# A decoder layer on one core: the last three value blocks worked quarter by quarter with a pre-summed second tile, gathered rows that end earlier, and four PSUM rooms for the queries

## The chip, the cores and the metric

The kernel runs on one core of a Trainium2 chip. The metric is device time in microseconds of one execution. The core has five engines with queues of their own: TensorE (PE, with its weight loads shown as PEld), VectorE (DVE), ScalarE (ACT), GpSimd (POOL) and SyncE (SP). DMA transfers are issued from the queues of SP and POOL here, and 16 DMA engines carry them.

## The reference, cut to what matters

One layer over 256 tokens of width 2048, in float32. An attention and retention part comes first (the first 575 us here, untouched by the change). Then a PEER block: product-key retrieval picks 16 of 16384 single-neuron experts for each of 8 heads of a token, so 128 experts a token.

```python
q = (hf @ w_q).reshape(T, PEER_HEADS, 2, PEER_QUERY_DIM // 2)
s_half = jnp.einsum('thpd,hpkd->thpk', q, sub_keys).astype(F32)
v_half, i_half = lax.top_k(s_half, K)
cand_s = (v_half[:, :, 0, :, None] + v_half[:, :, 1, None, :]).reshape(T, PEER_HEADS, K * K)
cand_i = (i_half[:, :, 0, :, None] * PEER_N_KEYS + i_half[:, :, 1, None, :]).reshape(T, PEER_HEADS, K * K)
top_s, pick = lax.top_k(cand_s, K)
experts = jnp.take_along_axis(cand_i, pick, axis=-1)
gates = jax.nn.softmax(top_s, axis=-1)
...
    a = jnp.einsum('cd,ced->ce', hc, w_u[ec]).astype(F32)
    coef = (gc * jax.nn.gelu(a)).astype(dt)
    return jnp.einsum('ce,ced->cd', coef, w_v[ec])
...
    x = x + gate2 * peer_ffn(h2, peer_w_q[l], peer_sub_keys[l], peer_u[l], peer_v[l])
return rmsnorm(x, g_norm_final)
```

## The kernel before

**Two ways to the experts.** Tokens 0 to 191 (TD = 192) go the dense way: all 16384 experts are computed on PE, and a matrix X holds gate times activation, which is zero for experts that a token didn't pick. The last 64 tokens (NS) go the sparse way: their 128 chosen rows are gathered from HBM by indirect DMAs on POOL, one 128x2048 tile a step, and DVE multiplies. Tokens 160 to 191 take their activations by gathering too (NM = 32). In all there are 160 steps: 32 "m", 64 "u" and 64 "v". They run beside the dense work, and `sparse(n)` says how many are due at a block; `STEPS` lists the blocks for three of the four dense stages. `most` is how many gathers may be in flight, `spare` and `other` are the rooms that they land in.

**Stages.** The expert matrices go in two halves of 64 blocks of 128 experts: first activation stage (`u_half`, hf = 0), first value stage (`v_group`, hf = 0), second activation stage, second value stage. Before them lies the query stage: 16 blocks of the query projection (`t_block`), each into a PSUM bank named by `bank("A")`, which goes round banks 6 and 7; then scores and top-16 on DVE.

**A value block (j).** SP loads 1 MB into one of five `raw` tiles (L148). ACT copies it, rounded, into `hi` (L946), DVE writes the rest, `lo = raw - hi` (L947). The block's slice of X is split likewise into `cc`: `ch` (L941), `cl` (L942) and a second copy of a part of `cl` (L948); `cc` has three buffers. PE then does 20 matmuls of 512 columns (L964) into eight accumulators, `acc[(t, q)]`, for token tile t and column quarter q, one PSUM bank each: three for a quarter of the first tile (hi by hi, hi by cl, lo by hi), two for a quarter of the second, whose rows 0 to 63 and 64 to 127 are two parts of the same 64 tokens and have to be added to each other at the end ("folded"). The first half's result waits in SBUF as `s2`.

**The end.** The last NL = 3 blocks are written by quarter: all of the nine (or six) matmuls of a quarter, then that quarter's finish. Blocks 62 and 63 have `hi` and `lo` in tiles of their own (`pair`). For the second tile the finish is `te = acc + s2` on DVE (L988, one buffer), two fp32 products with a 0/1 matrix `sel`, which fold the gathered rows' sum `sp` into rows 64 to 127 (L990) and `te` into rows 0 to 63 (L991), then, for both tiles, times the gate `g2` (L992), added to x in `z` (L993), squared and summed on ACT (L995), times `gf` (L996). After the fourth quarter of a tile follow the reciprocal root (L214, L215 on DVE, L220 on POOL), the scaling by it (ACT L1002, DVE L1004) and four output transfers on SP (L1005). `z` is the tile that held the activations' input; its two halves serve as rooms for gathers in the second value stage, and x is loaded into it from DRAM late (L929, on POOL). For the first tile `s2` is multiplied by `g2` (L931) and added to `z` (L933) ahead.

**What sets the order.** Program order gives priorities, and a list scheduler with a simulated timeline fixes the order of instructions on every engine before the program runs. Instructions passed through `pin` (`inorder` is `pin` from the fourth block on) keep their written order among themselves: the loads, ACT's copies for a block, the gathers and their DVE steps. Engines then run their queues strictly in that order. A tile is written again only when its last reader is done.

Of the kernel before, what the change touches and what calls it, by code (L numbers as in the profile page):

```python
# [9 lines left out]
F32 = mybir.dt.float32  # L10
# [34 lines left out]
             u1=[j for j in range(HALF - 8) if j % 3 != 1])  # L45
# [70 lines left out]
def body(ctx, tc, a, out, dbg=None, stop=None):  # L116
# [627 lines left out]
    with ExitStack() as gctx:  # L744
# [152 lines left out]
        def v_group(hf, s2, late, fin=None):  # L897
# [3 lines left out]
            with tc.tile_pool(name=f"vsb{hf}", bufs=1) as vb:  # L901
# [5 lines left out]
                if hf:  # L907

                    sel = vb.tile([P, 3 * NS], F32, name="sel")
                    nc.vector.memset(sel, 0.0)  # L910
                    nc.vector.tensor_add(sel[:, NS:2 * NS], ident[:, 0:NS], ident[:, NS:P])
                    z = x2
                    ss = vb.tile([P, 2, 4], F32, name="ss2")

                tail = HALF - (NL if hf else 1)
                last = []
                for j in range(HALF):
                    if hf == 1:
                        if j == 44:
                            other[0], most[0] = None, 2  # L920
                        elif j == 48:
# [3 lines left out]
                        elif j == 50:  # L925
                            most[0] = 1
                        elif j in (56, 57):
                            t = j - 56
                            nc.gpsimd.dma_start(z[:, t, :], x2d[:, t, :])  # L929
                        elif j == 58:  # L930
                            nc.vector.tensor_mul(s2[:, 0, :], s2[:, 0, :], g2)  # L931
                        elif j == 60:
                            nc.vector.tensor_add(z[:, 0, :], z[:, 0, :], s2[:, 0, :])  # L933
# [3 lines left out]
                    cc = gp_.tile([P, 2 * TD + NS], F32R, name="cc", bufs=3)  # L937
                    ch, cl = cc[:, 0:TD], cc[:, TD + NS:]

                    inorder = pin if j > 2 else lambda i: i  # L940
                    inorder(nc.scalar.copy(ch, xb(j)))  # L941
                    nc.vector.tensor_sub(cl, xb(j), ch.bitcast(F32))  # L942
# [4 lines left out]
                    nc.vector.tensor_sub(lo, r, hi.bitcast(F32))  # L947
# [15 lines left out]
                    def mul(c, jj, n, x, w, m):  # L963
                        nc.tensor.matmul(acc[c][0:m], x, w[:, c[1] * 512:(c[1] + 1) * 512], start=jj == 0 and n == 0,  # L964
                                         stop=jj == HALF - 1 and n == 2 - c[0], skip_group_check=True)

                    if j < HALF - 1:
# [6 lines left out]
                        continue  # L974
# [341 lines left out]
```

## Time and profile before

| | us |
|---|---|
| median of 3 runs (range) | 1890.0 (1884.99 to 1891.03) |
| the profiled execution, own time | 1895.85 |
| its span, first to last instruction | 1894.1 |
| PE busy | 1816.1 |
| DVE busy | 1479.9 |
| ACT busy | 708.7 |
| POOL busy | 379.5 |

All times inside the execution are counted from the start of the span. 0 to 575 is the attention part, 575 to 735 the queries, then the four expert stages begin at about 735, 986, 1279 and 1571. Every matmul of the activation stages is shown as two instructions, and so is each product with `sel`: they are float32. An instruction's duration includes its fill and drain, so several that follow each other start closer together than they last.

### The profile page before, as it was taken

Reading aid. Unit: us, or ns where it says so; the run is one execution under the profiler, and the core shown is the slowest. Engines: PE = TensorE matmul, PEld = TensorE weight load, DVE = VectorE, ACT = ScalarE, POOL = GpSimd, SP = SyncE. Lnnn points to the kernel's source line nnn. Section 1 sums busy time; section 2 is a strip of 40 time slices with the busy share of each in tenths; the row PEclk is TensorE's granted clock in tenths of the full one; section 3 lists DMA queues with packets and bytes.
Section 4 is the critical chain, followed back from the end, with each engine's and each line's share of the span. In section 5 each row is a group of like instructions: output and inputs, shape, how many; then the busy total and the mean of one; then the engine's idle time right before and its main releaser. Section 6 shows DMA issues by size and latency. Waiting matters only on the chain.

```text
span 1894.1 us, 28604 instructions
## 1 busy us (share of the span) xinstructions
PE 1816.1 (96%) x11303; PEld 1589.3 (84%) x11303; DVE 1479.9 (78%) x2333; ACT 708.7 (37%) x1279; POOL 379.5 (20%) x256
## 2 busy tenths in 40 slices
PE   5899999999997999999999999999999999999995
PEld 4899878788786899999997777779999997777773
DVE  7988877879788998778388999974455559888875
ACT  3444453625434422011035545541111114555552
POOL 1000001002001002111124444421111125544210
PEclk9999899989998999999999999999999999999998
DMA  8989876879887979999889999989989979999981
GB/s 350 388 323 373 309 274 231 311 258 349 298 321 276 339 278 342 424 395 355 356 320 406 422 417 413 416 337 425 367 330 355 366 301 421 422 413 387 383 294 45
DMA packets 94473, 652.93 MB, mean 345 GB/s; under 512 B 11409, under 2 KB 11617, under 8 KB 18433
## 3 DMA queue, kind: packets, MB, share of 16 engines
q1 hardware_dynamic: 66818, 467.78, 64.2%
q0 software_dynamic: 27520, 183.32, 24.2%
q8 instruction: 89, 1.46, 0.3%
q14 instruction: 46, 0.38, 0.1%
HBM read 644.97 MB, written 4.22 MB: 343 GB/s over the span
## 4 chain that ended last, share of the span: by engine, by line
PE 84%; DVE 9%; DMA 3%; issue 2%; ACT 1%; POOL 0%; SPq 0%; ACTq 0%; POOLq 0%; DVEq 0%
PE acc L964 31%; PE psU L1062 28%; PE psN L452 8%; PE psD L353 3%; DMA raw<-in_adaT 2%; PE bkB L353 2%; PE psA L236 2%; DVE raw L198 2%; DVE wlo L158 2%; PE pg L1047 1%; PE bkC L353 1%; PE bvB L405 1%; PE psA L237 1%; DMA raw<-in_winA 1%; PE pT L548 1%
## 5 line engine op out<-in xcount | busy, mean ns | idle before, releaser
L1062 PE MATMUL psU<-xT,raw 128*128 128x160 f32 x4096 | 569.9, 300 | 0.0
L1062 PEld LDWEIGHTS psU<-xT,raw 128*128 128x128 f32 x4096 | 558.3, 190 | 0.5
L964 PE MATMUL acc<-whi,cc 128*128 128x512 f32 x1512 | 367.8, 391 | 0.0
L964 PEld LDWEIGHTS acc<-whi,cc 128*128 128x128 f32 x1512 | 283.8, 188 | 68.9
L947 DVE TENSOR_TENSOR wlo<-raw,whi 128x2048 fp32r<-128x2048 f32 x126 | 288.2, 2288 | 63.6 <-issue 58.5
L964 PE MATMUL acc<-wlo,cc 128*128 128x512 f32 x1008 | 252.5, 391 | 0.6 <-DVE wlo L947 0.6
L946 ACT CAST whi<-raw 128x2048 fp32r<-128x2048 f32 x126 | 240.7, 1911 | 6.5 <-DMA raw<-in_v 6.5
L157 ACT CAST whi<-raw 128x1024 fp32r<-128x1024 f32 (+1 forms) x174 | 168.5, 1018 | 187.3 <-PE psN L452 43.8
L198 DVE SCALAR_TENSOR_TENSOR raw<-raw,crow 128x2048 f32<-128x2048 f32 x96 | 219.2, 2284 | 23.3 <-DMA raw<-in_adaT 23.2
L158 DVE TENSOR_TENSOR wlo<-raw,whi 128x1024 fp32r<-128x1024 f32 (+1 forms) x174 | 200.9, 1181 | 30.8 <-ACT whi L157 28.2
L964 PEld LDWEIGHTS acc<-wlo,cc 128*128 128x128 f32 x1008 | 162.0, 161 | 61.6 <-DVE wlo L947 1.3
L452 PE MATMUL psN<-whi,act 128*128 128x512 f32 x512 | 172.8, 414 | 1.3 <-ACT whi L157 1.1
L1068 DVE TENSOR_TENSOR X<-X,ge 128x160 f32<-128x160 f32 (+19 forms) x94 | 25.8, 276 | 165.3 <-ACT ge L1067 158.0
L1064 ACT ACTIVATE X<-psU 128x160 f32<-128x160 f32 (+19 forms) x102 | 25.6, 253 | 306.3 <-PE psU L1062 298.3
L452 PEld LDWEIGHTS psN<-whi,act 128*128 128x128 f32 x512 | 97.7, 194 | 26.9 <-issue 3.0
L452 PE MATMUL psN<-wlo,act 128*128 128x512 f32 x256 | 104.4, 410 | 3.6 <-DVE wlo L158 3.6
L941 ACT CAST cc<-X 128x192 fp32r<-128x192 f32 x128 | 44.8, 353 | 157.0 <-PE acc L964 155.9
L236 PE MATMUL psA<-act,whi 128*128 128x512 f32 x240 | 87.9, 407 | 3.2 <-ACT whi L157 3.2
L803 POOL DMA_INDIRECT rows<-in_urow,sx x32 | 71.8, 2244 | 91.6 <-DVE rows L844 76.3
L803 POOL DMA_INDIRECT s<-in_urow,sx x26 | 57.5, 2213 | 134.6 <-DVE s L844 101.9
L803 POOL DMA_INDIRECT xT<-in_v,sx x21 | 60.7, 2889 | 93.0 <-DVE cc L942 63.2
L844 DVE SCALAR_TENSOR_TENSOR rows<-rows,h2t 128x2048 f32<-128x2048 f32 x32 | 73.1, 2286 | 3.5 <-DMA rows<-in_urow,sx 3.5
(350 smaller groups left out, 2550.9 us busy)
## 6 DMA issues: line engine op xcount, KB each, us to landing
raw<-in_u SPq DMA_DIRECT2D x128, 1024.0 KB
raw<-in_v SPq DMA_DIRECT2D x128, 1024.0 KB
raw<-in_adaT SPq DMA_DIRECT2D x96, 1024.0 KB
raw<-in_winN SPq DMA_DIRECT2D x16, 1024.0 KB
raw<-in_woutN SPq DMA_DIRECT2D x16, 1024.0 KB
raw<-in_wqT SPq DMA_DIRECT2D x16, 1024.0 KB
raw<-in_winB SPq DMA_DIRECT2D x16, 832.0 KB
raw<-in_winD SPq DMA_DIRECT2D x12, 1024.0 KB
```

Source lines behind the costliest of these rows:

```text
L157: nc.scalar.copy(hi[:, sl], r[:, sl])
L158: nc.vector.tensor_sub(lo[:, sl], r[:, sl], hi[:, sl].bitcast(F32))
L198: nc.vector.scalar_tensor_tensor(r, r, 1.0, crow, op0=OP.mult, op1=OP.mult, accum_out=modc[:, j, k:k + 1])
L236: nc.tensor.matmul(p_, hi[:, sl], act[:, k], start=k == 0, stop=False, skip_group_check=True)
L353: nc.tensor.matmul(bank[:, b, :], x[:, w], y[:, k, :], start=k == k0 and n == 0 and first, stop=k == k1 - 1 and n == 2, skip_group_check=True)
L452: nc.tensor.matmul(ps[tt], x[:, k, ts_], y[:, w], start=k == 0 and j == 0, stop=k == KB - 1 and j == 2)
L803: pin(nc.gpsimd.indirect_dma_start(out=r, out_offset=None, in_=src, in_offset=bass.IndirectOffsetOnAxis(ap=o, axis=0)))
L844: pin(nc.vector.scalar_tensor_tensor(r, r, 1.0, h, op0=OP.mult, op1=OP.mult, accum_out=d[:, e:e + 1]))
L946: inorder(nc.scalar.copy(hi, r))
L947: nc.vector.tensor_sub(lo, r, hi.bitcast(F32))
L964: nc.tensor.matmul(acc[c][0:m], x, w[:, c[1] * 512:(c[1] + 1) * 512], start=jj == 0 and n == 0, stop=jj == HALF - 1 and n == 2 - c[0], ski ...
L1062: nc.tensor.matmul(ps, w[:, k * P:(k + 1) * P], xT[:, k, 0:TU], start=k == 0, stop=k == KB - 1)
```

## The change

It has three parts.

**Steps.** In the second activation stage the steps are those blocks below 52 whose number leaves a rest other than 1 by 4 (39 steps); before it was blocks below 56 with a rest other than 1 by 3 (37 steps). The room change at block 54 comes at 48. In the second value stage the remaining steps are spread over blocks 1 to 50 (before, 0 to 53), and the room changes and the loads of `g2` and `gf` come three blocks earlier.

**The end.** The second tile of `s2` is finished ahead, as the first was: two half-tile copies between partitions (on POOL, into the free `z`) bring the halves beside each other, two adds sum them, in rows 64 to 127 the gathered rows' sum, then follow the multiplication by `g2` and the add to `z`. So a quarter of the second tile needs only its accumulator copied to SBUF by ACT (into a `raw` tile) and one product with `sel`, which is issued behind the next quarter's matmuls (`folds`). These matmuls and products are pinned. `cc` for blocks 62 and 63 is made at block 59 in tiles of its own (`ccx`), and their `lo` is written in two halves. `tg` has three buffers, the square overwrites it, the fourth quarter's `gf` goes into its scaling, and the scaling and output order is 3, 0, 1, 2.

**Queries.** The query blocks go round four PSUM banks (6, 7, 2, 3).

```diff
-             u1=[j for j in range(HALF - 8) if j % 3 != 1])
+             u1=[j for j in range(HALF - 12) if j % 4 != 1])
...
-                    sel = vb.tile([P, 3 * NS], F32, name="sel")
+                    sel = vb.tile([P, P], F32, name="sel")
                     nc.vector.memset(sel, 0.0)
-                    nc.vector.tensor_add(sel[:, NS:2 * NS], ident[:, 0:NS], ident[:, NS:P])
+                    nc.vector.tensor_add(sel[:, 0:NS], ident[:, 0:NS], ident[:, NS:P])
...
-                        if j == 44:
+                        if j == 41:
                             other[0], most[0] = None, 2
-                        elif j == 48:
+                        elif j == 45:
                             g2, gf = fin()
                             row_load(g2, row5)
                             row_load(gf, a["gfin"])
-                        elif j == 50:
+                        elif j == 47:
                             most[0] = 1
-                        elif j in (56, 57):
-                            t = j - 56
-                            nc.gpsimd.dma_start(z[:, t, :], x2d[:, t, :])
+                        elif j == 52:
+                            nc.gpsimd.dma_start(z[0:NS, 0, :], s2[NS:P, 1, :])
+                            nc.gpsimd.dma_start(z[NS:P, 0, :], sps[0][0:NS, :])
+                            nc.gpsimd.dma_start(z[:, 1, :], x2d[:, 1, :])
+                        elif j == 53:
+                            nc.vector.tensor_mul(s2[:, 0, :], s2[:, 0, :], g2)
+                        elif j == 54:
+                            nc.vector.tensor_add(s2[0:NS, 1, :], s2[0:NS, 1, :], z[0:NS, 0, :])
+                        elif j == 55:
+                            nc.vector.tensor_add(s2[NS:P, 1, :], sps[0][NS:P, :], z[NS:P, 0, :])
+                            nc.gpsimd.dma_start(z[:, 0, :], x2d[:, 0, :])
+                        elif j == 56:
+                            nc.vector.tensor_mul(s2[:, 1, :], s2[:, 1, :], g2)
                         elif j == 58:
-                            nc.vector.tensor_mul(s2[:, 0, :], s2[:, 0, :], g2)
-                        elif j == 60:
-                            nc.vector.tensor_add(z[:, 0, :], z[:, 0, :], s2[:, 0, :])
+                            nc.vector.tensor_add(z[:, 1, :], z[:, 1, :], s2[:, 1, :])
...
+                    if j > tail:
+                        cc, cl = ccx.pop(0)
+                    else:
+                        cc, cl = activations(j, gp_.tile([P, 2 * TD + NS], F32R, name="cc", bufs=3))
...
-                    nc.vector.tensor_sub(lo, r, hi.bitcast(F32))
-                    inorder(nc.scalar.copy(cc[:, TD:TD + NS], cl[:, P:].bitcast(F32)))
+                    n = D // (1 + (j > tail))
+                    for i in range(0, D, n):
+                        nc.vector.tensor_sub(lo[:, i:i + n], r[:, i:i + n], hi[:, i:i + n].bitcast(F32))
+                    if j <= tail:
+                        inorder(nc.scalar.copy(cc[:, TD:TD + NS], cl[:, P:].bitcast(F32)))
                     last.append((j, hi, lo, cc))
+                    if hf and j == tail - 2:
+                        for i in range(tail + 1, HALF):
+                            ccx.append(activations(i, vb.tile([P, 2 * TD + NS], F32R, name="ccx", bufs=NL - 1)))
+                        for cx, lx in ccx:
+                            inorder(nc.scalar.copy(cx[:, TD:TD + NS], lx[:, P:].bitcast(F32)))
...
-                    elif j < tail:
-                        sparse(left[0] / max(1, 54 - j))
+                    elif 0 < j < tail:
+                        sparse(left[0] / max(1, 51 - j))
...
+                    def total(c, done):
+
+                        t, q = c
+                        sl = slice(q * 512, (q + 1) * 512)
+                        tg = vb.tile([P, 512], F32, name="tg", bufs=3)
+                        nc.vector.tensor_mul(tg, done, g2[:, sl])
+                        nc.vector.tensor_add(z[:, t, sl], z[:, t, sl], tg)
+                        nc.scalar.activation(tg, z[:, t, sl], AF.Square, accum_out=ss[:, t, q:q + 1])
+                        if q < 3:
+                            nc.vector.tensor_mul(z[:, t, sl], z[:, t, sl], gf[:, sl])
+                            return
+                        with tc.high_priority(offset=200):
+                            rc = token_rstd(vb, ss[:, t:t + 1, :], 1, f"rcf{t}")
+                        with tc.high_priority(offset=100 * t):
+                            for i in (3, 0, 1, 2):
+                                y = z[:, t, i * 512:(i + 1) * 512]
+                                if i == 3:
+                                    nc.vector.scalar_tensor_tensor(y, y, rc, gf[:, sl], op0=OP.mult, op1=OP.mult)
+                                elif i < 2:
+                                    nc.scalar.activation(y, y, AF.Copy, scale=rc)
+                                else:
+                                    nc.vector.tensor_scalar(y, y, rc, None, op0=OP.mult)
+                                nc.sync.dma_start(out[:, t, i * 512:(i + 1) * 512], y)
+
+                    if hf:
+                        nc.vector.tensor_add(z[:, 0, :], z[:, 0, :], s2[:, 0, :])
+                    folds = []
+
+                    def fold():
+
+                        c, e = folds.pop(0)
+                        done = up.tile([P, 512], F32, name="pc", tag=tag[c])
+                        pin(nc.tensor.matmul(done, sel, e, start=True, stop=True))
+                        total(c, done)
+
                     for c in chunks:
                         t, q = c
                         for jj, *p in last:
                             for n, p_ in enumerate(parts(t, *p)):
-                                mul(c, jj, n, *p_)
+                                i = mul(c, jj, n, *p_)
+                                if hf:
+                                    pin(i)
...
+                        if folds:
+                            fold()
                         if t:
-                            e = vb.tile([P, 512], F32, name="te", bufs=1)
-                            nc.vector.tensor_add(e, acc[c], s2[:, 1, sl])
-                            done = up.tile([P, 512], F32, name="pc", tag=tag[c])
-                            nc.tensor.matmul(done, sel[:, 0:P], sps[0][:, sl], start=True, stop=False)
-                            nc.tensor.matmul(done, sel[:, NS:NS + P], e, start=False, stop=True)
...
+                            e = chunk_tile("raw", F32)[:, 0:512]
+                            nc.scalar.copy(e, acc[c])
+                            folds.append((c, e))
+                        else:
+                            total(c, acc[c])
...
-        first = t_blocks(up, [wq(0), wq(1)], (bank("A"), bank("A")), 2)
+        qbank = lambda i: f"b{(6, 7, 2, 3)[i % 4]}"
+        first = t_blocks(up, [wq(0), wq(1)], (qbank(0), qbank(1)), 2)
         for i in range(16):
-            ps = first[i] if i < 2 else t_block(up, wq(i), bank("A"), dst=early if i == 2 else None)
+            ps = first[i] if i < 2 else t_block(up, wq(i), qbank(i), dst=early if i == 2 else None)
...
-                if j == HALF - 10:
+                if j == HALF - 10 - 6 * hf:
                     other[0], most[0] = more_room, 3 - hf
```

More of the change, by code (lines that the diff above doesn't have):

```diff
@@ L915, in v_group @@
                 tail = HALF - (NL if hf else 1)
-                last = []
+                last, ccx = [], []
                 for j in range(HALF):
                     if hf == 1:
-                        if j == 44:
+                        if j == 41:
                             other[0], most[0] = None, 2
-                        elif j == 48:
+                        elif j == 45:
                             g2, gf = fin()
@@ L930, in v_group @@
                         elif j == 58:
-                            nc.vector.tensor_mul(s2[:, 0, :], s2[:, 0, :], g2)
-                        elif j == 60:
-                            nc.vector.tensor_add(z[:, 0, :], z[:, 0, :], s2[:, 0, :])
+                            nc.vector.tensor_add(z[:, 1, :], z[:, 1, :], s2[:, 1, :])
                     elif j == 50:
                         spare[0], most[0] = None, 2
-                    cc = gp_.tile([P, 2 * TD + NS], F32R, name="cc", bufs=3)
-                    ch, cl = cc[:, 0:TD], cc[:, TD + NS:]
@@ L940, in v_group, with activations @@
                     inorder = pin if j > 2 else lambda i: i
-                    inorder(nc.scalar.copy(ch, xb(j)))
-                    nc.vector.tensor_sub(cl, xb(j), ch.bitcast(F32))
+                    def activations(j, cc):
+                        ch, cl = cc[:, 0:TD], cc[:, TD + NS:]
+                        inorder(nc.scalar.copy(ch, xb(j)))
+                        nc.vector.tensor_sub(cl, xb(j), ch.bitcast(F32))
+                        return cc, cl
+                    if j > tail:
+                        cc, cl = ccx.pop(0)
+                    else:
+                        cc, cl = activations(j, gp_.tile([P, 2 * TD + NS], F32R, name="cc", bufs=3))
@@ L963, in mul @@
                     def mul(c, jj, n, x, w, m):
-                        nc.tensor.matmul(acc[c][0:m], x, w[:, c[1] * 512:(c[1] + 1) * 512], start=jj == 0 and n == 0,
-                                         stop=jj == HALF - 1 and n == 2 - c[0], skip_group_check=True)
+                        return nc.tensor.matmul(acc[c][0:m], x, w[:, c[1] * 512:(c[1] + 1) * 512], start=jj == 0 and n == 0,
+                                                stop=jj == HALF - 1 and n == 2 - c[0], skip_group_check=True)
                     if j < HALF - 1:
```

16 lines of the change are left out of this document (removed).

## The prediction, made before the changed kernel was run

> **What bounds the kernel now.** I read the page first, then busy time by stage, then who TensorE (PE) waits for, and last the instructions in order of time at the end.
>
> ```profile
> span 1894.1 us, 28604 instructions
> PE 1816.1 (96%) x11303; PEld 1589.3 (84%) x11303; DVE 1479.9 (78%) x2333; ACT 708.7 (37%) x1279; POOL 379.5 (20%) x256
> ```
>
> PE is busy for 1816.1 of 1894.1 us, so only 78 us can be had without taking matmuls away. The next view says where they lie. Columns: stretch, length, busy time of PE, PE weight loads, DVE, ACT and POOL (instructions in brackets), granted PE clock, DMA share, GB/s.
>
> ```profile
> 575.00:660.00 85.00, 78.91 (x439) 67.21 (x439) 78.72 (x182) 44.13 (x73) 2.39 (x5) 0.93 0.83 299
> 660.00:735.00 75.00, 74.22 (x511) 70.21 (x510) 73.16 (x395) 19.18 (x39) 10.46 (x21) 1.00 0.79 283
> 986.00:1279.00 293.00, 293.00 (x1298) 227.02 (x1297) 260.02 (x220) 148.43 (x189) 115.58 (x46) 1.00 0.98 402
> 1279.00:1571.00 292.00, 292.00 (x2450) 291.04 (x2450) 151.85 (x246) 43.11 (x175) 51.83 (x39) 1.00 0.92 359
> 1571.00:1850.00 279.00, 278.39 (x1219) 215.25 (x1218) 242.68 (x162) 146.70 (x183) 106.44 (x40) 1.00 0.96 381
> 1850.00:1895.00 45.00, 21.83 (x79) 13.46 (x77) 24.98 (x40) 10.75 (x23) 1.13 (x2) 0.85 0.13 47
> ```
>
> The rows are the query stage (575 to 735), the first value stage, the second activation stage, the second value stage, and the end. From 735 to 1850 PE has nothing to gain but 0.6 us; in the last 45 us it works for 21.8. So the change is decided after 1850. The instructions there (start, duration, engine, line, operation, count, in brackets the idle time before and what ended it):
>
> ```profile
> 1842.72 0.35 DVE L942 TENSOR_TENSOR cc<-X,cc 128x192 fp32r<-128x192 f32 x1
> 1845.07 2.29 DVE L947 TENSOR_TENSOR wlo<-raw,whi 128x2048 fp32r<-128x2048 f32 x1 [2.00 <-issue]
> 1850.57 0.35 ACT L941 CAST cc<-X 128x192 fp32r<-128x192 f32 x1 [2.26 <-PE acc L964]
> 1850.83 1.90 ACT L946 CAST pair<-raw 128x2048 fp32r<-128x2048 f32 x1
> 1852.76 2.29 DVE L947 TENSOR_TENSOR pair<-raw,pair 128x2048 fp32r<-128x2048 f32 x1 [1.45 <-ACT pair L946]
> 1854.89 9.37 PE L964 MATMUL acc<-pair,cc 128*128 128x512 f32 x40
> 1854.97 2.28 DVE L933 TENSOR_TENSOR xT<-xT,s 128x2048 f32<-128x2048 f32 x1
> 1861.96 0.69 DVE L988 TENSOR_TENSOR te<-acc,s 128x512 f32<-128x512 f32 x1 [4.70 <-PE acc L964]
> 1864.09 1.02 PE L990 MATMUL pc<-sp,sel 128*128 128x512 f32 x2
> 1864.95 1.02 PE L991 MATMUL pc<-te,sel 128*128 128x512 f32 x2
> 1867.21 0.68 DVE L993 TENSOR_TENSOR xT<-xT,tg 128x512 f32<-128x512 f32 x1
> 1868.68 0.69 DVE L996 TENSOR_TENSOR xT<-xT,gf 128x512 f32<-128x512 f32 x1 [0.79 <-ACT sq L995]
> 1874.29 1.10 PE L990 MATMUL pc<-sp,sel 128*128 128x512 f32 x2 [1.47 <-DVE te L988]
> 1877.49 1.28 DVE L993 TENSOR_TENSOR xT<-xT,tg 128x512 f32<-128x512 f32 x2
> 1885.02 0.68 DVE L993 TENSOR_TENSOR xT<-xT,tg 128x512 f32<-128x512 f32 x1
> 1886.55 0.69 DVE L996 TENSOR_TENSOR xT<-xT,gf 128x512 f32<-128x512 f32 x1 [0.85 <-ACT sq L995]
> 1888.16 1.33 ACT L1002 ACTIVATE xT<-xT,rcf 128x512 f32<-128x512 f32 x2 [1.65 <-POOL rcf L220]
> 1888.16 0.88 DVE L1004 TENSOR_SCALAR xT<-xT,rcf 128x512 f32<-128x512 f32 x2 [0.67 <-POOL rcf L220]
> ```
>
> The last 40 matmuls of the value blocks run without a gap: (9.37-0.39)/39 = 0.230 us apart. The scheduler put block 61's 20 ahead of them, so the three-block tail starts at T0 = 1854.89 - 20 x 0.230 = 1850.3. No quarter was closed before 1861.96, though they are written quarter by quarter. Then the four quarters of the second tile go round in a ring, te on DVE, two products on PE, tg on DVE, 3.4 us each (1867.21 adds after the first round, 1874.29 starts the fourth), because te has one buffer; and all eight quarters' vector work follows. From the last value matmul (1864.3) to the end are 30 us.
>
> **The tail, part by part.** The matmuls of the last three blocks are pinned in the order written, so quarter (1,0) needs 6 matmuls and is closed at T0 + 1.4. The fold product of a quarter comes behind the next quarter's matmuls, fed by an ACT copy of the accumulator:
>
> ```profile
> L982 ACT COPY s<-acc x4: 587/590/592, 1276.0 to 1278.1; 128x512 f32<-128x512 f32 x4
> ```
>
> The same shape took 0.59 us, less than the 1.38 us of the next quarter: hidden; were it not, 0.6 us a quarter. The product with the gathered sum (L990) goes, four of eight. One such fp32 product takes 1864.95 - 1864.09 = 0.86 us. PE therefore ends at 1850.3 + 60 x 0.230 + 4 x 0.86 + 0.2 = 1867.7.
>
> On DVE a 512-wide operation follows the other by 0.60 us (two in 1.28). For the last quarter: multiply, then add from 1868.4. Before, from that add to the scaling took 1888.16 - 1885.02 = 3.14, with the 0.60 multiply by gf in between; that goes into the last scaling for the fourth quarters, so 2.54 remain: 1870.95. From the scaling to the end took 1894.1 - 1888.16 = 5.94, with as many operations and transfers as after: 1876.9. This is **-17.2 us**.
>
> What can eat into it. First, DVE's own load: from the arrival of (0,0) at 1860.6 to 1867.7 it must do 1.2 for (1,3), 0.4 for its reciprocal root, 0.69 and 0.44 for two of its scalings, and 5.4 for (0,0) to (0,2): 8.1 in 7.1. I take +1.0, from 0 to 1.5. Second, block 63's low part is now needed early: its first half by T0 + 4 x 0.23 = 1851.2. Before, ACT's cast of block 63 waited until 1850.57 for a cc buffer that PE had to free; the change computes the two blocks' activations ahead (four small casts, two 0.35 us subtractions, beside PE work that covers them: block 61's operands are ready 3 us ahead, so at worst 1 us) and lifts this wait. DVE then has, from the end of the subtraction for block 60 (1842.8) to 1851.2, 8.4 us for 2.29 + 2.29 + half of 2.29 + 0.35 = 6.1. There are 2.3 us to spare; one full-width operation (2.28) in between fits barely, two don't. I take +0.8, from 0 to 2.3.
>
> **The second tile's sum.** Two half-tile copies through POOL's queue, two adds, a multiply and an add over 2048 columns, 2.28 each (L933), replace the multiply and add for the first tile alone, which stay. Gate, x and copies wait for the last gathered step:
>
> ```profile
> 1781.32 2.29 DVE L931 TENSOR_TENSOR s<-s,g 128x2048 f32<-128x2048 f32 x1
> 1833.85 2.35 DVE L850 SCALAR_TENSOR_TENSOR sp<-xT,dots,sp 128x2048 f32<-128x2048 f32 x1
> xT<-x2d POOLq DMA_DIRECT2D x2, 1024.0 KB, 7.7
> xT<-in_v,sx POOLq DMA_INDIRECT x21, 14.0
> ```
>
> The last step ran at 1833.85. In this stage the steps are now spread to end three blocks sooner (51 for 54), at 20 x 0.230 = 4.6 us a block 13.8 us: the step would end at 1822.4. Copies take 7.7 us if like x2d's load, 14.0 if like a gather: 1830 to 1836; adds 4.6; x2d's reload of the first half waits for them (behind it on POOL only the final root); 7.7 to 14 more. DVE sits idle for 2.0 us a block there (the wait at 1845.07), four blocks, for four operations of 2.28: 9.1 in 8, covered but for the 0.8 already taken. L931 shows that the scheduler moves such work forward into gaps, L933 that it leaves a late one behind block 63.
>
> **Steps in the second activation stage.** 39 steps in 52 blocks instead of 37 in 56: 0.75 a block instead of 0.67. Two transfers of 1.05 MB: 1.75 x 1.05 in a block's 292 / 64 = 4.56 us are 402 GB/s. The first value stage has just that, 402 GB/s at 0.98 with PE at 293.00 of 293, also at three steps in four blocks; I take 0. From the other side, this stage's own row gives 359 / 0.92 = 390 GB/s at full share: 12 short over 237 us are 2.9 MB, 7.5 us if no prefetched block covers it. The second value stage gets 35 steps over 50 blocks, 0.70 against 0.69: nothing. Its start, where PE waited 0.6 us in 1571 to 1850, gains 0 to 0.6; I take 0.3.
>
> **Four query rooms.** PE's waits for it:
>
> ```profile
> PE psA L236 <- ACT whi L157: 3.2, 1, 3.2
> PE psA L236 <- ACT pair L157: 1.4, 1, 1.4
> PE psA L237 <- DVE wlo L158: 0.5, 1, 0.5
> ```
>
> They are for casts, not for rooms; DVE is busy 73.16 of 75 there and PE 74.22. 0 to 1.4 us; I take 0.4.
>
> **Sum:** -17.2 + 1.0 + 0.8 - 0.3 - 0.4 = -16.1. The profiled execution took 1895.85 us, 5.85 above the median 1890.0 of the runs; so 1879.8 for one like it, and a median of **1874**. Its own range: 1890 - 19.2 = 1871 to 1890 - 13.4 = 1877, and 1884 with the transfers' upper end.
>
> **Rivals.** (1) DVE works the quarters in strict order, waiting for each square. By the rows, add to gf takes 1.47 (1867.21 to 1868.68), with two operations 2.67 a quarter. Seven quarters from 1854.1, with 1.4 less for (1,3) and 1.5 for the first finish: 1872.9 instead of 1868.8. Time: -12, median 1878. For it: the 0.79 and 0.85 waits; against: at 1877.49 two adds stand together.
>
> (2) All five full-width operations land on DVE between blocks 60 and 63: 11.4 in 2.3 to spare, PE stalls 9.1 us and its clock falls. What that costs:
>
> ```profile
> 580.00:600.00 20.00, 15.95 (x74) 12.72 (x72) 14.39 (x23) 7.86 (x17) 0.00 (x0) 0.81 0.62 232
> ```
>
> After PE's idle time in 575 to 585 the granted clock was 0.81 over 20 us, 3.8 us lost. Together -16.1 - 0.8 + 9.1 + 3.8 = -4, median 1886. The Trainium skill, "TensorE: Matmul & The Clock Gate", section "Why this matters for your kernels", warns of PE gaps over some 3 us, after which it runs at half clock; this row agrees that the clock falls. By an estimate of one such window of 3.4 us at half clock from that page, 1.7 would be lost, and the median be 1884. The old tail's 1.5 us waits did not reach such a gap. Against the rival: L933 stood behind block 63.
>
> (3) Slower: the gathered steps don't end sooner, since near the end one gather is in flight at a time, at 14.0 us. Then the last step stays at 1836.2; copies 14.0, adds 4.6, reload 14.0, add 2.3: 1871. If the scheduler put these adds ahead of blocks 62 and 63 on DVE, their low parts wait behind transfers: 1871 + 3.4 = 1874.5 against 1851.2, 23.3 us of stall and 3.8 of clock: -16.1 - 0.8 + 27.1 = +10, median 1900. It is slower than before once block 63's first half comes after about 1864. For it: a gather's 14.0 us; against: the transfers' 7.7, and that room counts shrink three blocks sooner too. If DVE's order has them behind, it costs a few us as in (1).
>
> **Chances.** Forecast 0.65, (1) 0.17, (2) 0.11, (3) 0.07. Under 0.3% (5.7 us) no change can be told: 0.82 faster, 0.11 the same (2), 0.07 slower. The range runs from 1868 (the best sum less the 3 us by which runs scatter) to 1887, past (2)'s 1886, and leaves (3) out.
>
> **What would show it.** Group L988 gone, fold products half as many, no PE wait for DVE in the last 30 us; value matmuls and folds ending some 17 us after T0, the end some 9 us after these. The last gathered step about 13 us sooner; the second activation stage with PE at 292 of 292 and more DMA share. Wrong: PE waiting for pair (L947) in the tail means (2) or (3); squares ending most of DVE's idle time, (1); PE gaps before 1571, the transfers.

## The result, and the profile after

| | before | after |
|---|---|---|
| median of 6 runs, us (range) | 1888.88 (1884.99 to 1891.03) | 1874.73 (1872.07 to 1879.24) |
| ratio, 95% interval | | 0.9931 (0.9915 to 0.9947) |
| profiled execution, own time | 1895.85 | 1873.63 |
| its span | 1894.1 | 1871.8 |

On 1888.88 us the ratio is a gain of 13.0 us, between 10.0 and 16.1. The page of the kernel after (span, then busy time of the engines):

```profile
span 1871.8 us, 28573 instructions
...
PE 1806.5 (97%) x11295; PEld 1582.8 (85%) x11295; DVE 1485.9 (79%) x2333; ACT 709.4 (38%) x1283; POOL 369.2 (20%) x258
```

The spans differ by 22.3 us, and the ratio says 13, so the two profiled executions must not be subtracted as a whole. The instructions in order of time show the first query matmul of each (start, duration, engine, line, operation, count, the wait before). Before:

```profile
585.43 0.80 PE L236 MATMUL psA<-act,whi 128*128 128x512 f32 x1 [3.19 <-ACT whi L157]
```

After:

```profile
575.38 0.79 PE L236 MATMUL psA<-act,whi 128*128 128x512 f32 x1 [2.94 <-ACT whi L157]
```

Up to here both kernels issue the same instructions in the same order, and yet the second is 10.05 us ahead. Over the 14 profiled executions of this study this point lies anywhere between 573.87 and 587.08 us. It is scatter of the attention part and no effect of the change. What lies behind it can be compared stage by stage in the chain of waits (start, length, group of matmuls, count). Before:

```profile
985.93 292.31 PE acc L964 x1280
...
1577.84 286.41 PE acc L964 x1252
```

After:

```profile
976.12 292.31 PE acc L987 x1280
...
1568.04 263.54 PE acc L987 x1152
```

The two rows start the first and the second value stage. From the one to the other are 591.91 us before and 591.92 after: the new steps of the second activation stage cost and gain nothing. From the second row to the end of the span are 1894.1 - 1577.84 = 316.3 us before and 1871.8 - 1568.04 = 303.8 after. **All of the gain that the trace shows, 12.5 us, lies in the second value stage**, which the ratio's interval holds. This length, the "last stage" from here on, doesn't contain the scatter of the attention part, and it is the measure for the experiments beside the ratio.

The end of the kernel after, in order of time:

```profile
1810.38 2.35 DVE L850 SCALAR_TENSOR_TENSOR sp<-xT,dots,sp 128x2048 f32<-128x2048 f32 x1
...
1826.17 2.29 DVE L964 TENSOR_TENSOR wlo<-raw,whi 128x2048 fp32r<-128x2048 f32 x1 [1.91 <-ACT ccx L950]
...
1828.76 0.52 ACT L972 CAST ccx<-ccx 128x64 fp32r<-128x64 f32 x2 [3.42 <-DVE ccx L951]
1829.03 2.29 DVE L936 TENSOR_TENSOR s<-sp,xT 64x2048 f32<-64x2048 f32 x1
...
1829.44 1.90 ACT L961 CAST whi<-raw 128x2048 fp32r<-128x2048 f32 x1
...
1831.63 2.29 DVE L939 TENSOR_TENSOR s<-s,g 128x2048 f32<-128x2048 f32 x1
...
1833.83 2.29 DVE L964 TENSOR_TENSOR wlo<-raw,whi 128x2048 fp32r<-128x2048 f32 x1
...
1836.30 2.29 DVE L941 TENSOR_TENSOR xT<-xT,s 128x2048 f32<-128x2048 f32 x1
...
1838.50 2.29 DVE L964 TENSOR_TENSOR wlo<-raw,whi 128x2048 fp32r<-128x2048 f32 x1
...
1839.61 1.09 PE L987 MATMUL acc<-whi,cc 128*128 128x512 f32 x4
1840.70 4.63 DVE L964 TENSOR_TENSOR pair<-raw,pair 128x1024 fp32r<-128x1024 f32 x4
...
1840.85 0.44 PE L987 MATMUL acc<-wlo,cc 128*64 128x512 f32 x1
...
1841.98 0.68 PE L987 MATMUL acc<-pair,ccx 128*64 128x512 f32 x2 [0.46 <-DVE pair L964]
...
1844.25 0.68 PE L987 MATMUL acc<-pair,ccx 128*64 128x512 f32 x2 [1.59 <-DVE pair L964]
...
1845.24 2.30 DVE L1023 TENSOR_TENSOR xT<-xT,s 128x2048 f32<-128x2048 f32 x1
...
1847.26 0.39 PE L987 MATMUL acc<-whi,cc 128*128 128x512 f32 x1
...
1859.40 1.56 PE L987 MATMUL acc<-pair,ccx 128*128 128x512 f32 x6
...
1862.40 0.69 DVE L1003 TENSOR_TENSOR tg<-acc,g 128x512 f32<-128x512 f32 x1
...
1863.12 0.69 DVE L1004 TENSOR_TENSOR xT<-xT,tg 128x512 f32<-128x512 f32 x1
...
1865.67 1.34 ACT L1017 ACTIVATE xT<-xT,rcf 128x512 f32<-128x512 f32 x2 [1.04 <-POOL rcf L220]
```

The rows are, from above: the last gathered step; the low part of block 59; the copies for `ccx` on ACT, which waited 3.42 us for DVE; the second of the two adds that sum the second tile's halves; ACT's cast of block 60, behind those copies; the multiply by the gate; the low part of block 60; the second tile's add to x; the low parts of blocks 61, 62 and 63; the tail's first matmul and two waits of PE for low parts; the first tile's add to x; a matmul of the third quarter, behind the first fold product; PE's last matmuls, which end at 1860.96; and the last quarter's multiply, add and scaling.

The tail starts where the four matmuls of 1839.61 end, at 1839.61 + 4 x 0.230 = 1840.53. From there to the end are 31.3 us; before they were 1894.1 - 1850.3 = 43.8. PE's matmuls now reach over 20.4 of these 31.3 us, with the quarters' vector work beside them.

### The profile page after: what moved, and what is told of

Read it like the earlier page. It is cut to its first block, busy times and chain, and to the rows that moved or that the text cites. A ratio compares the mean times of both kernels' runs of the same rounds, so it can differ in the third digit from the quotient of the medians.

```text
span 1871.8 us, 28573 instructions
## 1 busy us (share of the span) xinstructions
PE 1806.5 (97%) x11295; PEld 1582.8 (85%) x11295; DVE 1485.9 (79%) x2333; ACT 709.4 (38%) x1283; POOL 369.2 (20%) x258
## 4 chain that ended last, share of the span: by engine, by line
PE 82%; DVE 8%; issue 4%; DMA 3%; ACT 1%; POOL 0%; SPq 0%; ACTq 0%; POOLq 0%; DVEq 0%
PE acc L987 30%; PE psU L1108 28%; PE psN L452 6%; PE psD L353 3%; PE bkB L353 2%; PE psA L236 2%; DVE wlo L158 2%; DVE raw L198 2%; PE pg L1093 1%; DMA raw<-in_adaT 1%; PE bkC L353 1%; PE psA L237 1%; DMA raw<-in_winA 1%; PE bvB L405 1%; PE pT L548 1%
## 5 line engine op out<-in xcount | busy, mean ns | idle before, releaser
L353 PE MATMUL psD<-act,whi 128*128 128x256 f32 x384 | 74.8, 295 | 0.6 <-ACT whi L157 0.6
```

The lines of the kernel that those rows point to most:

```text
L353: nc.tensor.matmul(bank[:, b, :], x[:, w], y[:, k, :], start=k == k0 and n == 0 and first, stop=k == k1 - 1 and n == 2, skip_group_check=True)
```

## The experiments

Each kernel has its edit, its ratio to the kernel before, and its last stage, worked out as above from the chain and span of its one profiled execution:

| kernel | what it is | ratio (95% interval) | last stage, us |
|---|---|---|---|
| before | | 1 | 316.3 |
| after | the whole change | 0.9931 (0.9915 to 0.9947) | 303.8 |
| e1 | before + four query rooms | 1.0000 (0.9989 to 1.0011) | 316.3 |
| e3 | before + the new steps | 1.0006 (0.9992 to 1.0019) | 316.3 |
| e9 | before + quarter matmuls in written order | 1.0002 (0.9989 to 1.0015) | 316.6 |
| e8 | before + four buffers for `te` | 0.9976 (0.9963 to 0.9989) | 312.0 |
| e4 | after without the written order | 0.9966 (0.9953 to 0.9978) | 309.5 |
| e2 | after without rooms and second activation stage's steps | 0.9961 (0.9947 to 0.9974) | 308.0 |
| e11 | after without the second activation stage's steps | 0.9940 (0.9923 to 0.9958) | 307.6 |
| e5 | after, three full-width adds on GpSimd | 0.9968 (0.9954 to 0.9982) | 310.9 |
| e10 | after, all events of the second value stage three blocks sooner | 0.9929 (0.9914 to 0.9944) | 303.8 |
| e12 | e10 + `ccx` at block 40 | 0.9914 (0.9899 to 0.9928) | 302.6 |
| e13 | e10 + low parts ahead of the first tile's add | 0.9920 (0.9901 to 0.9939) | 301.6 |
| e14 | both | 0.9930 (0.9915 to 0.9945) | 300.7 |

The last stage came out the same for the three kernels that end alike (before, e1, e3), and every ratio's interval holds the gain in the last stage. The intervals reach 2 to 4 us to either side, so differences of a few us between two of these kernels rest on the last stage.

### The parts, each alone (e1, e2, e3)

```diff
# e1 = before with
+        qbank = lambda i: f"b{(6, 7, 2, 3)[i % 4]}"
...
-            ps = first[i] if i < 2 else t_block(up, wq(i), bank("A"), dst=early if i == 2 else None)
+            ps = first[i] if i < 2 else t_block(up, wq(i), qbank(i), dst=early if i == 2 else None)
# e3 = before with
-             u1=[j for j in range(HALF - 8) if j % 3 != 1])
+             u1=[j for j in range(HALF - 12) if j % 4 != 1])
...
-                        if j == 44:
+                        if j == 41:
...
-                        elif j == 48:
+                        elif j == 45:
...
-                        elif j == 50:
+                        elif j == 47:
...
-                    elif j < tail:
-                        sparse(left[0] / max(1, 54 - j))
+                    elif 0 < j < tail:
+                        sparse(left[0] / max(1, 51 - j))
# e2 = after with
-             u1=[j for j in range(HALF - 12) if j % 4 != 1])
+             u1=[j for j in range(HALF - 8) if j % 3 != 1])
...
-            ps = first[i] if i < 2 else t_block(up, wq(i), qbank(i), dst=early if i == 2 else None)
+            ps = first[i] if i < 2 else t_block(up, wq(i), bank("A"), dst=early if i == 2 else None)
```

In e3 and e2 the block of the room change in the second activation stage goes with the steps, and in e1 and e2 the first two query blocks (`first`) go by the same rooms as the others.

> The kernel before with the four query rooms alone. Theory (the whole gain is made after the last value block starts): within 3 us of before, and the query stage, from the first query matmul to the first activation matmul of the unbroken row, 144 us as in the profiles of before (585.4 to 729.7) and after (575.4 to 720.1), within 1 us. Rival (the rooms let PE run ahead of DVE's copies): 3 to 8 us faster, with that stage shorter by as much.

> The kernel before with the gathered rows' steps alone: the second activation stage's 39 steps by block 51, the second value stage's steps by block 50 and its room changes three blocks earlier; the old tail stays. Theory: within 3 us of before; the last gathered step about 13.7 us earlier, second activation stage 292 us. Rival (earlier steps free DMA and DVE before the tail): 4 us faster or more. Second rival (0.75 transfers more a block starve PE): up to 7.5 us slower with PE idle in the second activation stage.

> The changed kernel with the second activation stage's steps and the two query rooms of before: the tail and the value stage's steps alone. Theory: as the changed kernel, 14 us faster than before, within 3 us. Rival (rooms and steps bring half): 6 to 9 us faster.

The rooms do nothing, and the steps by themselves do nothing, though in e3 the last gathered step comes 13.7 us sooner within its stage. The tail alone should then have given all of it, as I expected, and gave 8.3 of 12.5 us. That is the size of the rival (rooms and steps bring half). Its end, in order of time:

```profile
1846.50 2.35 DVE L964 TENSOR_TENSOR pair<-raw,pair 128x1024 fp32r<-128x1024 f32 x2
...
1848.77 2.28 DVE L941 TENSOR_TENSOR xT<-xT,s 128x2048 f32<-128x2048 f32 x1
...
1850.97 2.35 DVE L964 TENSOR_TENSOR pair<-raw,pair 128x1024 fp32r<-128x1024 f32 x2
...
1852.24 1.11 PE L987 MATMUL acc<-pair,ccx 128*64 128x512 f32 x2 [3.79 <-DVE pair L964]
...
1853.16 0.63 PE L987 MATMUL acc<-wlo,cc 128*64 128x512 f32 x1
...
1855.72 1.70 PE L1030 MATMUL pc<-raw,sel 128*128 128x512 f32 x2
...
1857.49 0.40 PE L987 MATMUL acc<-whi,cc 128*128 128x512 f32 x1
```

The scheduler put the second tile's add to x (L941) between the low parts of blocks 62 and 63, where the kernel after has it ahead of block 61. So PE waits 3.79 us instead of 1.59, and behind the wait the same matmuls last longer: two take 1.11 where they took 0.68 in the kernel after, and a fold product, which takes 1.02 in quiet times, 1.70. From the end of its long wait to the `whi` matmul behind the first fold product e2 needs 1857.49 - 1852.24 = 5.25 us, the kernel after 1847.26 - 1844.25 = 3.01. The granted clock was 0.54 over this stretch of e2, and 1.00 in the kernel after. The wait costs 2.2 more, the slower clock behind it another 2.2: together 4.4, for the 4.2 us by which the last stages differ. This is the prediction's rival (2), on one operation instead of five.

### Which part set that order (e11)

```diff
# e11 = after with (rooms stay at four)
-             u1=[j for j in range(HALF - 12) if j % 4 != 1])
+             u1=[j for j in range(HALF - 8) if j % 3 != 1])
-                if j == HALF - 10 - 6 * hf:
+                if j == HALF - 10:
```

> The changed kernel with only the second activation stage's steps of before (37 in 56 blocks), query rooms as changed. Theory (these steps cost nothing where they are, but the scheduler's order at the end hangs on them: with the old ones the add of the second tile to x stands on DVE between blocks 62 and 63): last stage 308.0 us as with both old, PE waiting 3.8 us for block 63 and the matmuls behind it at 0.6 instead of 0.4 us each; the second activation stage 292 us. Rival (the rooms or DMA made the difference): last stage 303.8.

As expected, 307.6, with the same wait of 3.8, and with L941 between the low parts of blocks 62 and 63 as in e2. It isn't that the gathered rows end later: the last gathered step starts 242.3 us into the last stage, in e11 as in the kernel after. So the steps of the second activation stage, which cost nothing and gain nothing where they stand, are worth 3.8 us at the end, because the order of DVE's instructions comes out otherwise there.

### What the tail's own parts are worth (e4, e8, e9)

```diff
# e4 = after with
-                        pin(nc.tensor.matmul(done, sel, e, start=True, stop=True))
+                        nc.tensor.matmul(done, sel, e, start=True, stop=True)
-                                i = mul(c, jj, n, *p_)
-                                if hf:
-                                    pin(i)
+                                mul(c, jj, n, *p_)
# e8 = before with
-                            e = vb.tile([P, 512], F32, name="te", bufs=1)
+                            e = chunk_tile("raw", F32)[:, 0:512]
# e9 = before with
-                                mul(c, jj, n, *p_)
+                                i = mul(c, jj, n, *p_)
+                                if hf:
+                                    pin(i)
```

> The kernel before with te in a raw tile of its own for each quarter instead of one buffer, nothing else. Theory (the ring of te, products and tg sets the pace of 3.4 us a quarter from 1864 on, but behind it stands DVE with 17 us of work that can't start before 1862): PE's 4.4 us of waits for te go, the last stage is 311 to 313 us, 3 to 5 us faster than before. Rival (the ring is the whole gain): 306 or less. Second rival (DVE was the bound already): 315 or more.

> The kernel before with the matmuls of the last three blocks pinned in the written order by quarter, nothing else. Theory (the order is worth little without the activations made ahead, the presum and a te of its own for each quarter): PE waits some 4 us for block 63, whose cast waits for a cc buffer, and then 1 us or more a quarter for te; last stage 310 to 315 us, 2 to 6 us faster than before. Rival (the order alone is the gain): 306 or less.

> The changed kernel with the matmuls and fold products of the last three blocks not pinned, so that the scheduler orders them, and it puts blocks before quarters and all four fold products last. Theory (the written order is needed beside the presum: without it DVE gets its first quarter late): PE waits less for low parts, yet the last stage is 306 to 309 us, 2 to 5 us longer than the changed kernel. Rival (the presum and single product are the gain, the pinned order only costs waits): 303 or less.

In e8 the four `te` follow each other without waiting for the products:

```profile
1850.51 2.48 DVE L988 TENSOR_TENSOR raw<-acc,s 128x512 f32<-128x512 f32 x4 [4.70 <-PE acc L964]
```

The ring of waits is gone, and that is worth 4.3 us: DVE then works without a longer pause to the end, so what is left behind the matmuls is its own work for eight quarters. In e9 the order is as written, and it is worth nothing. PE's waits for DVE there (sum, count, longest):

```profile
PE pc L992 <- DVE te L990: 5.5, 4, 2.2
...
PE acc L964 <- DVE pair L947: 3.7, 1, 3.7
```

I had expected 310 to 315; it took 316.6. Quarters that are closed early gain nothing while PE still waits for the one `te` buffer four times and 3.7 us for block 63's low part. In e4 the second tile is summed ahead but the order is free:

```profile
1856.42 3.60 PE L1030 MATMUL pc<-raw,sel 128*128 128x512 f32 x8
1857.48 0.69 DVE L1003 TENSOR_TENSOR tg<-pc,g 128x512 f32<-128x512 f32 x1 [7.97 <-PE pc L1030]
```

PE waits for nothing, but all folds come last, and DVE idles 7.97 us before the first quarter's multiply. 309.5 is 6.8 us less than before, 5.7 more than after; I had expected 306 to 309. So the rest of the change without the order gives 6.8, the order without the rest nothing, both 12.5: the order pays only together with the rest. A buffer of its own for each `te` gives 4.3 by itself (e8). What the pre-sum, the activations made ahead and the halved low parts are worth one by one was not tried.

### The adds on GpSimd (e5)

```diff
# e5 = after with
-                            nc.vector.tensor_add(s2[0:NS, 1, :], s2[0:NS, 1, :], z[0:NS, 0, :])
+                            nc.gpsimd.tensor_add(s2[0:NS, 1, :], s2[0:NS, 1, :], z[0:NS, 0, :])
# and the same in the adds of L936 and L941
```

> The changed kernel with the two adds of the second tile's sum and its add to x on GpSimd instead of VectorE. Theory (PE's 2.6 us of waits in the tail, for low parts of blocks 61 to 63, come from these operations standing before them on DVE): the waits fall to under 1 us, the tail from the last three blocks' first matmul to the end is 2 to 3 us shorter than the changed kernel's 31, so some 16 us faster than before. Rival (the waits come from the casts' order or from the activations made ahead): waits unchanged, same time as the changed kernel. Second rival (GpSimd's additions slow DVE or come too late, being slower than DVE's 2.3 us): slower than the changed kernel by 2 us or more.

The last stage grew by 7.1 us, as in the second rival. GpSimd and DVE in order of time, and PE's wait behind them:

```profile
1821.89 6.52 POOL L936 TENSOR_TENSOR s<-sp,xT 64x2048 f32<-64x2048 f32 x1 [2.85 <-DMA xT<-sp]
...
1823.86 4.77 DVE L951 TENSOR_TENSOR cc<-X,cc 128x192 fp32r<-128x192 f32 x1
...
1838.60 6.47 POOL L941 TENSOR_TENSOR xT<-xT,s 128x2048 f32<-128x2048 f32 x1 [9.31 <-DVE s L939]
...
1840.63 8.93 DVE L964 TENSOR_TENSOR pair<-raw,pair 128x1024 fp32r<-128x1024 f32 x4
...
1846.21 1.11 PE L987 MATMUL acc<-pair,ccx 128*64 128x512 f32 x2 [4.76 <-DVE pair L964]
```

A subtraction of 192 columns, which takes 0.35 us elsewhere, took 4.77, and ended at 1828.6, just when GpSimd's add did (1821.89 + 6.52 = 1828.4). The four subtractions for blocks 62 and 63 took 8.93 where they take 4.63; the 4.3 more are the 1838.60 + 6.47 - 1840.63 = 4.4 us for which GpSimd's second add still ran. So DVE stood still while GpSimd added. GpSimd had waited first: the add of 1838.60 began while DVE's subtraction for block 61 still ran, from 1838.43 to 1840.71, and ended 4.4 us after that. By this estimate the add itself takes some 4.4 us, and 2.1 of its 6.47 are waiting. The Trainium skill, "SBUF — State Buffer", section "Who interferes with whom", says that a DVE instruction with two SBUF inputs contends with a GpSimd instruction that reads SBUF, and that the order of issue decides which of the two blocks; these rows agree.

### Where the missing 3 us are (e10, e12, e13, e14)

The forecast for this stage was -15.4 (-17.2 + 1.0 + 0.8), and PE's waits for low parts are what it did not have. First theory: the second tile's operations come too late.

```diff
# e10 = after with all events of the second value stage three blocks sooner
-                        if j == 41:
+                        if j == 38:
...
-                        elif j == 58:
+                        elif j == 55:
...
-                        sparse(left[0] / max(1, 51 - j))
+                        sparse(left[0] / max(1, 48 - j))
# e12 = e10 with
-                    if hf and j == tail - 2:
+                    if hf and j == 40:
# e13 = e10 with
-                        nc.vector.tensor_sub(lo[:, i:i + n], r[:, i:i + n], hi[:, i:i + n].bitcast(F32))
+                        s_ = nc.vector.tensor_sub(lo[:, i:i + n], r[:, i:i + n], hi[:, i:i + n].bitcast(F32))
+                        if hf and j > tail:
+                            pin(s_)
-                        nc.vector.tensor_add(z[:, 0, :], z[:, 0, :], s2[:, 0, :])
+                        pin(nc.vector.tensor_add(z[:, 0, :], z[:, 0, :], s2[:, 0, :]))
# e14 = e12 and e13
```

> The changed kernel with every event of the second value stage three blocks earlier (steps spread to block 48, second tile's sum at blocks 49 to 55). The last stage, from its first long row of value matmuls to the end, took 316.3 us before, 303.8 in the changed kernel. Theory (PE's 2.6 us of waits in the tail come from the second tile's operations standing on DVE ahead of the low parts of blocks 60 to 63): these operations now stand before blocks 56 to 60, the waits for low parts of blocks 61 to 63 fall under 0.6 us and the last stage to 300.5 to 301.5; 3 us under the changed kernel, some 16 under before. Rival (DVE is the bound of the tail whatever PE waits for): waits gone, last stage 303 or more. Second rival (fewer blocks for the same gathers): PE starves before the tail, last stage over 304.

That theory fell: 303.8, the same waits. The end of e10, ACT and DVE:

```profile
1835.57 0.52 ACT L972 CAST ccx<-ccx 128x64 fp32r<-128x64 f32 x2 [3.92 <-DVE ccx L951]
...
1840.66 2.29 DVE L1023 TENSOR_TENSOR xT<-xT,s 128x2048 f32<-128x2048 f32 x1
...
1842.86 2.29 DVE L964 TENSOR_TENSOR wlo<-raw,whi 128x2048 fp32r<-128x2048 f32 x1
1845.06 4.63 DVE L964 TENSOR_TENSOR pair<-raw,pair 128x1024 fp32r<-128x1024 f32 x4
```

The freed place was taken at once: the first tile's add (L1023), which stood behind block 63 in the kernel after, went ahead of block 61. And ACT's copies for `ccx`, which keep their written order, still wait nearly 4 us, with block 60's cast queued behind them, and DVE's subtraction for block 60 behind that cast. Two candidates, so the next three kernels take away the one, the other, and both.

> The kernel with every event of the second value stage three blocks earlier, and in it the activations of blocks 62 and 63 made at block 40 instead of block 59. Its last stage took 303.8 us with PE waiting 2.9 us for low parts, no better than the changed kernel. New theory: two things hold DVE there, each enough by itself. ACT's pinned copies for the activations made ahead wait 3.9 us for DVE, with the cast of block 60 queued behind them; and the first tile's add to x (2.3 us) stands ahead of the low parts of 62 and 63. With the first gone and the second in place the waits go down by some 1 us, last stage 302.5 to 303.2. Rival (the activations made ahead are the whole cause): waits under 0.8 us, 301.5 or less. Second rival (they have no part): 303.8.

> The kernel with every event three blocks earlier, and in it the low parts of blocks 62 and 63 and the first tile's add to x pinned in this order, so that the add stands behind them; the activations made ahead stay at block 59. New theory: last stage 301.5 to 302.3, since block 60's cast is still late. Rival (the add has no part): 303.8.

> The kernel with every event three blocks earlier, the activations of blocks 62 and 63 made at block 40, and the first tile's add to x pinned behind the low parts. New theory: PE waits for low parts under 0.6 us, last stage 300.5 to 301.3, 3 us under the changed kernel; the whole some 16 us faster than before. Rival (DVE is the bound of the tail, whatever PE waits for): waits gone, last stage 303 or more.

In the last stage all three came out as expected: 302.6, 301.6 and 300.7, that is 1.2, 2.2 and 3.1 us less than e10. In e14 PE waits for no low part in the tail:

```profile
1847.90 4.63 DVE L964 TENSOR_TENSOR pair<-raw,pair 128x1024 fp32r<-128x1024 f32 x4
...
1850.00 1.09 PE L989 MATMUL acc<-whi,cc 128*128 128x512 f32 x4
1850.93 0.40 PE L989 MATMUL acc<-wlo,cc 128*64 128x512 f32 x1
...
1852.44 2.29 DVE L1025 TENSOR_TENSOR xT<-xT,s 128x2048 f32<-128x2048 f32 x1
...
1866.91 1.56 PE L989 MATMUL acc<-pair,ccx 128*128 128x512 f32 x6
...
1869.81 0.69 DVE L1005 TENSOR_TENSOR tg<-acc,g 128x512 f32<-128x512 f32 x1
```

The low parts of 62 and 63 start 3 us ahead of the tail, and PE needs 1866.91 + 1.56 - 1850.92 = 17.55 us for it. So the waits are explained by two causes whose costs nearly add: ACT's copies for `ccx`, held by DVE, and full-width operations ahead of the last low parts. These runs start from e10; in the kernel after the full-width operations are L936, L939 and L941, and its own share of the two causes was not tried by itself.

Whether e12, e13 or e14 beats the kernel after in the whole time the runs don't settle: the four intervals overlap, and e14, for which I had expected some 16 us in the whole, has a ratio that gives 13.2. By the last stage e14 is 3.1 us ahead, but its profiled execution reached the queries at 587.08, 11.7 us later than that of the kernel after, and a 3 us gain is hidden by such scatter.

## Why the prediction was right

The time (1874, measured 1874.73) and the sign were right, and the mechanism was. That the time came out within 1 us is luck in part. The sum said -16.1, at the edge of the measured 10.0 to 16.1, and the trace shows -12.5: 2.9 us too much in this stage, and 0.7 for the rooms and the stage's start, which gave nothing. The base hid 1.1 us of this, since three runs gave 1890.0 for the kernel before and six give 1888.88; the two medians, which differ by 14.2 us, hid another 1.7. Of the 2.9 us, 2.2 are PE's waits, 0.5 DVE's load and 0.2 the last transfers, as follows.

**The tail's matmuls and the chain behind them (-17.2): right.** Without waits PE needs 17.55 us for the tail (e14), predicted 1867.7 - 1850.3 = 17.4. From the last quarter's add to the scaling: 1865.67 - 1863.12 = 2.55, predicted 2.54. From the scaling to the end: 6.1, predicted 5.94. The ring through `te` was named as a cost before; by itself it is worth 4.3 (e8).

**DVE's load at the last quarter (+1.0, from 0 to 1.5): right, near the end of its range.** The last multiply starts 1862.40 - 1860.96 = 1.44 us after PE's end; 1.34 in e14.

**Block 63's low part (+0.8, from 0 to 2.3): the step that failed.** PE's tail took 1860.96 - 1840.53 = 20.4 us, 2.9 more than in e14; 2.4 of it are seen as waits (1.59, 0.46, and 0.3 for block 61's low part). The step counted 8.4 us of DVE's time, from the end of block 60's subtraction, for 6.1 of work, and let one full-width operation in. One stood there indeed (L941). But the starting point was taken from the kernel before, where block 60's subtraction ended at 1842.8:

```profile
1840.51 2.29 DVE L947 TENSOR_TENSOR wlo<-raw,whi 128x2048 fp32r<-128x2048 f32 x1 [1.84 <-issue]
```

The second value stage starts 9.8 us earlier in the kernel after, which makes it 1833.0; it ended at 1836.1. The 3.1 us before it had been used by L936 and L939, which stand together between blocks 59 and 60, while ACT's held `ccx` copies kept block 60's cast back. 3.1 and 2.3 against 2.3 to spare leave 3.1 late, and 2.9 was lost. The prediction had costed the activations ahead at nothing, at worst 1 us, "beside PE work that covers them"; PE's work does cover them, but the casts behind them in ACT's queue come late. Which part of the 2.9 us is ACT's and which DVE's is known for e10 alone (1.2 and 2.2, e12 and e13).

**The second tile's sum: its transfers right, its place on DVE wrong.** The DMA issues of the last 92 us (count, KB each, median us to landing):

```profile
xT<-x2d POOLq DMA_DIRECT2D x2, 1024.0 KB, 8.3
...
xT<-s POOLq DMA_DIRECT2D x1, 512.0 KB, 6.0
xT<-sp POOLq DMA_DIRECT2D x1, 512.0 KB, 6.0
```

The copies took 6.0 us, less than the 7.7 to 14.0 allowed. They did not both wait for the last gathered step, as the prediction had it: the one from `s2` was issued at 1804.16, before that step, and only the one from `sp` at 1813.02, behind it. The last gathered step came at 1810.38, against 1833.85 - 9.8 = 1824.05 before: 13.7 us sooner, predicted 13.8. Rival (3) needed it not to move. That the four operations go into four gaps, one to a block, and are covered was wrong: two of them (L936, L939) stand between blocks 59 and 60, and this is part of the waits above.

**Steps in the second activation stage (0, at worst 7.5 us): right by itself** (591.91 and 591.92 us), but what they do to the order at the end, 3.8 us (e11), was not thought of. The 0.3 us for the start of the second value stage did not show: the stages before it are equally long.

**The rooms (0.4): nothing to be seen** (e1). From the first query matmul to the start of the unbroken row of the first activation stage's matmuls the profiled executions take 143.4 to 144.9 us, with either number of rooms, so 0.4 could not be told from 0.

**The rivals.** (1), strict order with waits for each square: no; DVE's waits for a square are 0.79 us at most, and its first fold's multiply stands at 1847.44. (2), full-width operations ahead of 63: half true in the kernel after. PE did wait for `pair`, the prediction's own sign for (2) or (3), but for 2 us and with a granted clock of 1.00. It is seen in full in e2 and e11; in e5 the wait has another cause, the adds on GpSimd. Its price for the clock, 3.8 us behind a stall of 9.1, was not tried; it was taken over 20 us of a row, though PE's first query matmul starts only at 585.43; from there to 600 a granted clock of 0.81 takes 2.8. Behind the shorter wait of e2 the price was 2.2. The Trainium skill's "TensorE: Matmul & The Clock Gate", section "Why this matters for your kernels", had given 1.7 by the estimate in the prediction, which is nearer to that.

## What to carry to other kernels

A finish that runs piece by piece beside the matmuls needs both the order written out and pieces that don't wait for one buffer or a late operand: the order alone gave 0 here, the rest alone 6.8 us, together 12.5. When work is moved ahead of a tail, count what it pushes back on each queue it joins, from the new place of the neighbours and not from their old times; and look through the scheduler's order at the end after any edit, however far away. Where the front of a kernel scatters by more than the effect, compare the length of the stage that was changed, from one trace to the other.

## What the runs showed of the hardware

- The same instructions of the attention part took 573.87 to 587.08 us up to the first query matmul, over 14 profiled executions.
- A 128x2048 float32 add took 6.47 us on GpSimd, 2.1 of them waiting for a DVE subtraction, and 2.29 on DVE. DVE's instructions with two SBUF inputs stood still behind it (in e5 0.35 became 4.77 us), so an add moved away from DVE, where it takes 2.29, cost DVE 4.4 us.
- PE's waits of 1.6 us (after, e12) left the matmuls behind them at 0.40 us. Waits of 3.8 and 4.8 us (e2, e5) were followed by 4.9 us, and by 8.0 us with a second wait of 1.2 in them, at a granted clock of 0.50, with matmuls of 0.63, and in e2 a fold product of 1.70 instead of 1.02. The Trainium skill, "TensorE: Matmul & The Clock Gate", section "Why this matters for your kernels", puts the limit at a gap of some 3 us; these rows agree.
